# Mixer projections one weight tile at a time in one bank each, neighbourhood scores in the projections' banks, products of two heads side by side

## The chip, the cores and the metric

The kernel runs on one core of a Trainium2 chip. The metric is the device time of one execution in microseconds (us); the figure for a kernel is the median of several executions. One further execution is taken by the hardware profiler, and all views of the trace come from it.

## The reference: what is computed

Two layers of a macaron encoder over 512 tokens of width 1024, in float32: half a SwiGLU step, a mixer, half a SwiGLU step, and a last RMSNorm. Only the mixer is touched by the change. It projects the normalised input once, splits the result, and runs two groups of heads side by side: eight heads of neighbourhood attention (NA) on an 8 x 64 grid with a learned bias, and four heads of gated linear attention (GLA) in both directions.

```python
def hybrid_layer(x, ...):
    x = x + 0.5 * swiglu(rmsnorm(x, ffn1_norm), ffn1_wg, ffn1_wu, ffn1_wd)
    h = rmsnorm(x, mix_norm)
    proj = h @ w_in
    na_q, na_k, na_v, g_q, g_k, g_v, g_r, gf_code, gb_code = jnp.split(proj, offsets, axis=-1)
    na_o = neighbourhood_attention(split_heads(na_q, NA_HEADS), split_heads(na_k, NA_HEADS),
                                   split_heads(na_v, NA_HEADS), na_rpb)
    na_o = rmsnorm(merge_heads(na_o), na_gain)
    ...
    o_fwd = gla_chunked(qg, kg, vg, log_gf, True)
    o_bwd = flip(gla_chunked(flip(qg), flip(kg), flip(vg), flip(log_gb), False))
    gla_o = rmsnorm(o_fwd + o_bwd, gla_gain).astype(x.dtype)
    gla_o = merge_heads(gla_o) * jax.nn.silu(g_r)
    x = x + jnp.concatenate([na_o, gla_o], axis=-1) @ w_out
    x = x + 0.5 * swiglu(rmsnorm(x, ffn2_norm), ffn2_wg, ffn2_wu, ffn2_wd)
    return x
```

## The kernel before

A float32 product is made of three passes (`mm3`): weights and activations are split into a high and a low part, and high by high, high by low and low by high are added up in one PSUM bank. ACT rounds the high part of a weight tile (L149, the tile `wh`), DVE subtracts it to get the low part (L150, `wl`), and the matmuls stand on lines L169 to L171. Moving tiles are 512 tokens wide.

Each layer runs FFN 1, the mixer and FFN 2 one after the other. In the mixer, `mixer` builds four streams and hands them to `interleave`, which steps through generators: each step yields a price and a delay, or the name of a result that it waits for, and the stream that is due first is stepped next. This gives the instructions a priority; a list scheduler then puts every engine's instructions in their order when the program is built. The four streams are `gla_all(0)` and `gla_all(1)` (two GLA heads each), `na_all` (eight units of NA, two heads by half the queries each) and `fillers`: the projections of the remaining eleven pairs of 128-column weight tiles in the order of `PAIRS`, then the NA half of the output projection (`op_part`, eight chunks).

`fillers` are the large products, 128x128 weights by 512 columns, that keep TensorE busy while the other streams wait for ACT and DVE. A pair is made by `dmat_steps`: two weight tiles in two banks of the tag "mm", their k-steps alternating, or by `vmat_steps` for the NA values, whose rows are tokens. When the last k-step of both is issued, `posts[...]` evacuates both banks. The tag "mm" is a ring of four PSUM banks, used for projections, for the sum of `gla_out` and for the output projection; the tag "sc" is a ring of two banks, used for the scores of GLA and of NA.

The small products take part of the array. GLA scores are 16 products of 64x64 for two heads (L630, two passes each, so 32 matmul records), 8 of 64x128 at n=128 (L701) and two blocks of 4 at n=256 (L715). A unit of NA takes 4 products of 64x128 at n=256 for its scores (L853), bias, row maximum and sum on DVE, exponentials on ACT (L865), four transposes (L876), and 8 products of 128x64 with the values (L887, P·V below). The values are copied to `M_v` with a scale per token (L808) and shifted copies `M_vm` are made of them (L813, L814). `gla_out` sums a GLA head (L769 to L773), squares and copies the bank on ACT (L776, L777), sums the squares over partitions on TensorE (L236, L237), and multiplies by the root and by Silu of the gate `gr` (L744) on DVE. The last chunks of the output projection carry tile names with OP.

Of the kernel before, what the change touches and what calls it, by code (L numbers as in the profile page):

```python
# [13 lines left out]
ALU = mybir.AluOpType  # L14
# [49 lines left out]
def trunk_kernel(ctx, tc, xin, wgu, wdn, win, wcode, wgate, wout, vec, rpbt,  # L64
# [102 lines left out]

    def mm3(ps, wh, wl, rh, rl, first, last, more=False):
        PE.matmul(ps, wh, rh, start=first, stop=False, skip_group_check=more)  # L169
        PE.matmul(ps, wh, rl, start=False, stop=False, skip_group_check=more)  # L170
        PE.matmul(ps, wl, rh, start=False, stop=last, skip_group_check=more)  # L171

# [150 lines left out]
    def dload(src, eng):  # L323
        raw = wp.tile([P, 2048], F32, tag="wraw", name=nm("wraw"))
        for q in (1, 0, 2, 3):
            qs = slice(q * T, (q + 1) * T)
            eng.dma_start(raw[:, qs], src[:, qs])
# [205 lines left out]
    def mixer(l):  # L533
# [58 lines left out]
        def post_gqk(pr):  # L592
            def post(ok, oq, r):
                for key, o in (("gk", ok), ("gq", oq)):
                    t = got[key, pr] = sl(key)
                    V.tensor_tensor(seq_out(t), unit_in(o), unit_in(r), op=ALU.mult)
            return post

        def gla_levels(pr):
# [49 lines left out]
            for li, h in enumerate((1, 2, 4, 8, 16, 32, 64, 128)):  # L649
# [45 lines left out]
                elif h2 == 128:  # L695
                    pss = psum("sc"), psum("sc")
                    for s in range(4):
                        t = s ^ 1
                        kk, qq = (KF, QF) if s < t else (KB, QB)
                        for hh in range(2):  # L700
                            PE.matmul(pss[hh][:, s * P:(s + 1) * P], kk[rows[hh], s * P:(s + 1) * P],  # L701
                                      qq[rows[hh], t * P:(t + 1) * P], start=True, stop=True)
# [4 lines left out]
                else:  # L707
                    for half in range(2):
# [3 lines left out]
                        for j in range(2):  # L712
                            s = 2 * half + j
                            for hh in range(2):
                                PE.matmul(pss[hh][:, j * 256:(j + 1) * 256],  # L715
                                          kk[rows[hh], s * P:(s + 1) * P], qq[rows[hh], o:o + 256],
                                          start=True, stop=True)
# [5 lines left out]
        def post_gv(h0):  # L723
            def post(o1, o2, r):
                vts = sl("vt"), sl("vt")
                for vt, o in zip(vts, (o1, o2)):
                    V.tensor_tensor(seq_out(vt), unit_in(o), unit_in(r), op=ALU.mult)

                def turn():
                    for hd, vt in zip((h0, h0 + 1), vts):  # L730
                        pt = psum("tp")
                        for i in range(4):
                            PE.transpose(pt[:, i * P:(i + 1) * P], vt[:, i * P:(i + 1) * P], idn)
                        got["gv", hd] = sl("gv")
                        S.activation(got["gv", hd], pt, AF.Copy)
# [3 lines left out]
        def post_gr(h0):  # L739
            def post(o1, o2, r):  # L740
# [12 lines left out]
        def gla_out(hd, tag):  # L753
            g = gla[hd // 2]
            hh = hd % 2
            yield ("gr", hd)
# [31 lines left out]
        def vmat_steps(pss, src, tags):  # L788
# [3 lines left out]
            pss += [psum(tag) for tag in tags]  # L792
            for t in range(4):
                ps = pss[t // 2][:, (t % 2) * H2:(t % 2 + 1) * H2]
                ts = slice(t * P, (t + 1) * P)
# [355 lines left out]
```

## Time and profile before

| | |
|---|---|
| median of 3 executions | 1952.68 us (1950.92 to 1956.05) |
| the profiled execution | 1957.23 us, of which the span of instructions 1955.5 us |
| busy share of the span | TensorE 98%, its weight loads 86%, VectorE 72%, ScalarE 52%, GpSimd 1% |
| mixer of layer 0 | about 370 to 630 us |
| mixer of layer 1 | about 1337 to 1600 us |

TensorE's matmuls are pipelined, so the busy time of one is longer than the distance to the next one; the distance of two starts is what a matmul costs. The granted clock of TensorE is given as a share of its full rate. All rows are in the section below the change.

### The profile page before, as it was taken

What the parts mean: (1) busy time and instruction counts of PE and PEld (TensorE: products, weight loads), DVE (VectorE), ACT (ScalarE), POOL (GpSimd) and SP (SyncE); (2) the same over time, 40 slices, a digit from 0 to 9 for tenths busy, and PEclk for the clock granted to TensorE, in tenths of its full rate; (3) what the DMA queues carried; (4) which work ended last, traced back from release to release, by engine and by line L of the source; (5) the groups of instructions that cost most, each with busy time, mean ns of one, the idle gap of its engine ahead of it and who ended that gap; (6) DMA issues with size and microseconds to landing.
All of it is one profiled execution on the core that took longest, in us unless ns stands there. A gap on an engine that the chain in (4) does not pass through costs nothing.

```text
span 1955.5 us, 32220 instructions
## 1 busy us (share of the span) xinstructions
PE 1924.7 (98%) x12490; PEld 1687.4 (86%) x12490; DVE 1416.9 (72%) x2705; ACT 1020.1 (52%) x1959; POOL 17.4 (1%) x36
## 2 busy tenths in 40 slices
PE   8999999999998999999999999999999999999997
PEld 7889989888777898999889899988887778999896
DVE  6958768676558875967788596776764689679585
ACT  5535536465564553644555364455654655546364
POOL 0000000000000000000000000000000000000000
PEclk9999999999999999999999999999999899999999
DMA  4333223322202332332223333232221033233322
GB/s 154 112 108 108 89 106 124 110 67 98 66 31 85 102 108 89 106 108 103 83 98 106 108 109 107 88 119 96 96 86 55 21 120 107 89 107 109 108 76 76
DMA packets 58249, 187.78 MB, mean 96 GB/s; under 512 B 6640, under 2 KB 13296, under 8 KB 45808
## 3 DMA queue, kind: packets, MB, share of 16 engines
q1 hardware_dynamic: 29904, 132.07, 19.8%
q10 hardware_dynamic: 25632, 45.27, 7.0%
q0 software_dynamic: 2560, 8.39, 1.3%
q8 instruction: 98, 1.61, 0.3%
q14 instruction: 55, 0.45, 0.1%
HBM read 183.60 MB, written 2.10 MB: 95 GB/s over the span
## 4 chain that ended last, share of the span: by engine, by line
PE 97%; DVE 1%; DMA 1%; ACT 1%; issue 0%; DVEq 0%; ACTq 0%
PE F_mm L169 14%; PE F_mm L171 14%; PE F_mm L170 14%; PE F_sc L169 9%; PE F_sc L170 9%; PE F_sc L171 9%; PE M_mm L169 6%; PE M_mm L170 6%; PE M_mm L171 6%; PE M_o L887 1%; PE M_sc L630 1%; PE M_tp L876 1%; PE M_sc L853 1%; PE M_mm L773 1%; PE M_sc L715 1%; DMA wraw<-in_wgu 0%
## 5 line engine op out<-in xcount | busy, mean ns | idle before, releaser
L149 ACT ACTIVATE F_wh<-F_wraw 128x512 fp32r<-128x512 f32 (+1 forms) x472 | 289.5, 617 | 439.9 <-PE F_sc L170 238.8
L169 PE MATMUL F_mm<-F_xc,F_wh 128*128 128x256 f32 x1792 | 500.5, 282 | 1.3 <-ACT F_wh L149 1.3
L170 PE MATMUL F_mm<-F_xc,F_wh 128*128 128x256 f32 x1792 | 501.5, 282 | 0.0
L171 PE MATMUL F_mm<-F_xc,F_wl 128*128 128x256 f32 x1792 | 495.2, 282 | 0.0
L150 DVE TENSOR_TENSOR F_wl<-F_wraw,F_wh 128x512 fp32r<-128x512 f32 (+1 forms) x472 | 312.8, 668 | 151.9 <-ACT F_wh L149 143.4
L169 PEld LDWEIGHTS F_mm<-F_xc,F_wh 128*128 128x128 f32 x1792 | 339.3, 190 | 3.7 <-ACT F_wh L149 1.9
L170 PEld LDWEIGHTS F_mm<-F_xc,F_wh 128*128 128x128 f32 x1792 | 340.3, 190 | 1.9
L171 PEld LDWEIGHTS F_mm<-F_xc,F_wl 128*128 128x128 f32 x1792 | 335.8, 190 | 0.0
L169 PE MATMUL F_sc<-F_hid,F_wh 128*128 128x512 f32 (+1 forms) x716 | 275.6, 387 | 1.3 <-DVE xt L455 1.3
L170 PE MATMUL F_sc<-F_hid,F_wh 128*128 128x512 f32 (+1 forms) x716 | 276.6, 386 | 0.0
L171 PE MATMUL F_sc<-F_hid,F_wl 128*128 128x512 f32 (+1 forms) x716 | 276.4, 386 | 0.0
L149 ACT ACTIVATE F_wh<-F_ws 128x512 fp32r<-128x512 f32 x256 | 161.8, 632 | 170.0 <-PE F_mm L170 109.8
L150 DVE TENSOR_TENSOR F_wl<-F_ws,F_wh 128x512 fp32r<-128x512 f32 x256 | 174.8, 688 | 41.8 <-ACT F_wh L149 38.8
L169 PEld LDWEIGHTS F_sc<-F_hid,F_wh 128*128 128x128 f32 x716 | 134.6, 188 | 29.0 <-DVE xt L455 3.0
L171 PEld LDWEIGHTS F_sc<-F_hid,F_wl 128*128 128x128 f32 x716 | 134.5, 188 | 26.4
L170 PEld LDWEIGHTS F_sc<-F_hid,F_wh 128*128 128x128 f32 x716 | 134.6, 188 | 25.7
L455 DVE SCALAR_TENSOR_TENSOR xt<-F_sc,xt 128x512 f32<-128x512 f32 x94 | 65.0, 691 | 96.7 <-PE F_sc L171 96.1
L169 PE MATMUL M_mm<-F_xd,M_wh 128*128 128x512 f32 x304 | 122.1, 403 | 0.0
L171 PE MATMUL M_mm<-F_xd,M_wl 128*128 128x512 f32 x304 | 120.3, 397 | 0.0
L170 PE MATMUL M_mm<-F_xd,M_wh 128*128 128x512 f32 x304 | 119.9, 395 | 0.0
L150 DVE TENSOR_TENSOR M_wl<-M_wraw,M_wh 128x512 fp32r<-128x512 f32 (+1 forms) x112 | 73.4, 669 | 35.9 <-ACT M_wh L149 32.4
L149 ACT ACTIVATE M_wh<-M_wraw 128x512 fp32r<-128x512 f32 (+1 forms) x112 | 67.6, 614 | 46.8 <-PE M_mm L170 37.9
(325 smaller groups left out, 3153.0 us busy)
## 6 DMA issues: line engine op xcount, KB each, us to landing
F_wraw<-in_wgu SPq DMA_DIRECT2D x64, 1024.0 KB, 4.7
F_wraw<-in_wdn SPq DMA_DIRECT2D x32, 1024.0 KB, 4.9
M_wraw<-in_win ACTq DMA_DIRECT2D x88, 256.0 KB, 3.6
F_wraw<-in_wgu ACTq DMA_DIRECT2D x80, 256.0 KB, 3.8
F_wraw<-in_wdn SPq DMA_DIRECT2D x16, 768.0 KB, 4.3
M_pp<-in_rpbt POOLq DMA_DIRECT2D x32, 256.0 KB, 3.1
M_wraw<-in_wout SPq DMA_DIRECT2D x16, 256.0 KB, 2.7
xt<-in_xin SPq DMA_DIRECT2D x8, 256.0 KB, 5.2
```

What stands on the lines that cost most here:

```text
L149: S.activation(h, src, AF.Copy)
L150: V.tensor_tensor(l, src, h.bitcast(F32), op=ALU.subtract)
L169: PE.matmul(ps, wh, rh, start=first, stop=False, skip_group_check=more)
L170: PE.matmul(ps, wh, rl, start=False, stop=False, skip_group_check=more)
L171: PE.matmul(ps, wl, rh, start=False, stop=last, skip_group_check=more)
L455: V.scalar_tensor_tensor(xt[:, c, :], pss[j], 0.5, xt[:, c, :], ALU.mult, ALU.add)
L630: PE.matmul(pss[hh][o:o + 64, (i // 2) * 64:(i // 2 + 1) * 64], *op(hh, i), start=True, stop=True)
L715: PE.matmul(pss[hh][:, j * 256:(j + 1) * 256], kk[rows[hh], s * P:(s + 1) * P], qq[rows[hh], o:o + 256], start=True, stop=True)
L773: PE.matmul(dst, vs(2 * half + j), fa[:, o:o + P], start=False, stop=(j == 1))
L853: PE.matmul(sco[hh][:, jj * 256:(jj + 1) * 256], q[rows[hh], j * P:(j + 1) * P], krhs, start=True, stop=True)
L876: PE.transpose(pt[:, i * P:(i + 1) * P], pp[:, i * P:(i + 1) * P], idn)
L887: PE.matmul(po[rows[hh], j * P:(j + 1) * P], v[:, rows[hh]], pps[hh][:, (jj * 2 + c) * P:(jj * 2 + c + 1) * P], start=(c == 0), stop=(c == 1))
```

## The change

Five things change in the mixer.

- `paired` is new: it issues the products of two heads in turn, head 1 then head 0, and asks for program order for all but the first of a group. GLA scores, NA scores and P·V go through it, so in the new file their matmuls all stand on L171, and `mm3` on L176 to L178.
- The NA scores take two banks of the tag "mm" in place of "sc".
- Projections go by `tile_steps`: 24 matmuls of one weight tile in one bank, which is evacuated at once by `done`, then the other tile. The pieces of a weight tile are fetched in another order. `vmat_steps` also works bank by bank. The prices of a step are 1.36 and 1.5 in place of 1.28.
- The posts handle one tile each. Silu of both gates comes when the second is there, and `gla_out` waits for a new key "gs".
- The wait of NA for the values moves from the start of a unit to just before its P·V.

```diff
+    def paired(mms):
+        for i, (ps, lhs, rhs, kw) in enumerate(mms):
+            ins = PE.matmul(ps, lhs, rhs, **kw)
+            if i:
+                tc.keep_in_program_order(ins)
...
-    def dload(src, eng):
+    def dload(src, eng, order=(1, 0, 2, 3)):
...
             def blocks(pss, op):
-                for i in range(8):
-                    o = (i % 2) * 64
-                    for hh in range(2):
-                        PE.matmul(pss[hh][o:o + 64, (i // 2) * 64:(i // 2 + 1) * 64], *op(hh, i),
-                                  start=True, stop=True)
+                paired([(pss[hh][i % 2 * 64:i % 2 * 64 + 64, (i // 2) * 64:(i // 2 + 1) * 64], *op(hh, i), SS)
+                        for i in range(8) for hh in (1, 0)])
...
         def post_gr(h0):
-            def post(o1, o2, r):
-                for hd, o in ((h0, o1), (h0 + 1, o2)):
-                    g = got["gr", hd] = sl("gr")
-                    V.tensor_tensor(g, o, r, op=ALU.mult)
-                    S.activation(g, g, AF.Silu)
-                lnexp()
+            def post(i, o, r):
+                g = got["gr", h0 + i] = sl("gr")
+                V.tensor_tensor(g, o, r, op=ALU.mult)
+                if i == 1:
+                    for hd in (h0, h0 + 1):
+                        S.activation(got["gr", hd], got["gr", hd], AF.Silu)
+                    lnexp()
+                    got["gs", h0] = got["gs", h0 + 1] = True
...
-        def vmat_steps(pss, src, tags):
+        def vmat_steps(src, done):
...
+        def tile_steps(src, done):
+            raw = dload(src, nc.scalar, (1, 2, 0, 3))
+            for j, qs in enumerate(((1, 2), (0, 3))):
+                w = [wsplit(raw[:, q * T:(q + 1) * T]) for q in qs]
+                ps = psum("mm")
+                for c in range(KD):
+                    h, l_ = w[c % 2]
+                    cs = slice(c // 2 * P, (c // 2 + 1) * P)
+                    mm3(ps, h[:, cs], l_[:, cs], *XD[c], c == 0, c == KD - 1)
+                    if c == KD - 1:
+                        done(j, ps)
+                    if c % 2:
+                        yield 1.36, 0.0
...
         def na_unit(hp, jp, pps, ctxd):
-            sco = psum("sc"), psum("sc")
+            sco = psum("mm"), psum("mm")
...
+            paired([(sco[hh][:, jj * 256:(jj + 1) * 256],
+                     q[rows[hh], (2 * jp + jj) * P:(2 * jp + jj + 1) * P], keys(hh, 2 * jp + jj), SS)
+                    for jj in range(2) for hh in (1, 0)])
...
             if jp == 0:
+                yield ("v", hp)
                 ctxd["po"] = psum("o")
...
+            paired([(po[rows[hh], j * P:(j + 1) * P], got["v", hp][VSEL[j][c]][:, rows[hh]],
+                     pps[hh][:, (j % 2 * 2 + c) * P:(j % 2 * 2 + c + 1) * P], dict(start=c == 0, stop=c == 1))
+                    for j in (2 * jp, 2 * jp + 1) for c in range(2) for hh in (1, 0)])
...
                     yield ("qk", u // 2)
-                    yield ("v", u // 2)
...
-                steps = (vmat_steps if a in ("v0", "v2") else dmat_steps)(bk, win[l, i], ("mm", "mm"))
+                steps = vmat_steps if a in ("v0", "v2") else tile_steps
```

The orders below are those of the two built programs; a row is an instruction, `xN` counts repetitions.

TensorE before, where the projections of a layer end (tiles 5800 and 5801 are the last two, `F_xd` is the mixer's input, 5762 is the P·V sum of the last NA heads):

```order
L170 MATMUL M_mm_5801<-F_xd_3834,M_wh_5823 128x512
L171 MATMUL M_mm_5801<-F_xd_3834,M_wl_5824 128x512
L630 MATMUL M_sc_5700<-M_ga_4630 64x64 x8
L630 MATMUL M_sc_5701<-M_ga_4630 64x64 x8
L876 MATMUL M_tp_5734<-con,M_pp_5501 128x128 x4
L701 MATMUL M_sc_5865<-M_ga_4630 128x128 x4
L701 MATMUL M_sc_5866<-M_ga_4630 128x128 x4
L876 MATMUL M_tp_5750<-con,M_pp_5503 128x128 x4
L887 MATMUL M_o_5762<-M_pp_5501,M_vm_4993 64x128
L715 MATMUL M_sc_6005<-M_ga_4630 128x256 x2
```

TensorE after, at the end of the P·V of the last NA heads (5643 there):

```order
L171 MATMUL M_o_5643<-M_pp_5390,M_v_4992 64x128
L171 MATMUL M_o_5643<-M_pp_5388,M_v_4992 64x128
L176 MATMUL M_mm_5715<-F_xd_3605,M_wh_5707 128x512
L177 MATMUL M_mm_5715<-F_xd_3605,M_wh_5707 128x512
L178 MATMUL M_mm_5715<-F_xd_3605,M_wl_5708 128x512
L176 MATMUL M_mm_5715<-F_xd_3611,M_wh_5711 128x512
```

Before, the last NA unit, the last GLA scores and the sums of all four GLA heads stand behind the last projection; after, tile 5715 and three more tiles (5784, 5842 and 5995), 96 matmuls in all, stand behind the last P·V.

TensorE after, the first NA unit's P·V inside a group of GLA scores (4510 and 4509 are the score banks of two GLA heads, 4484 is the first P·V sum):

```order
L171 MATMUL M_sc_4510<-M_ga_4167,M_kt_4402 64x64
L171 MATMUL M_sc_4509<-M_ga_4167,M_kt_4402 64x64
L171 MATMUL M_o_4484<-M_pp_4090,M_vm_4452 64x128
L171 MATMUL M_o_4484<-M_pp_4088,M_vm_4452 64x128
L171 MATMUL M_o_4484<-M_pp_4090,M_vm_4452 64x128
L171 MATMUL M_o_4484<-M_pp_4088,M_vm_4452 64x128
L171 MATMUL M_sc_4510<-M_ga_4167,M_kt_4402 64x64
L171 MATMUL M_sc_4509<-M_ga_4167,M_kt_4402 64x64
```

ACT after, ahead of the shifted values 4452 that these P·V products read (4343 is the bank of the values):

```order
L907 ACTIVATE M_pp_4116<-M_tp_4430 128x512
L336 DMA M_wraw_4882<-in_win 128x512
L149 ACTIVATE M_wh_4698<-M_wraw_4693 128x512
L336 DMA M_wraw_4882<-in_win 128x512
L895 ACTIVATE M_pp_4309,M_sm_4412<-M_pp_4309,M_sm_4412 128x256 x2
L895 ACTIVATE M_pp_4311,M_sm_4418<-M_pp_4311,M_sm_4418 128x256 x2
L832 ACTIVATE M_v_4337<-M_mm_4343,rcol 128x128
L832 ACTIVATE M_v_4338<-M_mm_4343,rcol 128x128
L832 ACTIVATE M_v_4337<-M_mm_4343,rcol 128x128
L832 ACTIVATE M_v_4338<-M_mm_4343,rcol 128x128
L149 ACTIVATE M_wh_4702<-M_wraw_4693 128x512
L840 ACTIVATE M_vm_4452<-M_v_4337 64x384
```

A group of 16 is cut in two by P·V, four products of which read shifted values that ACT makes behind the exponentials of the next NA unit.

TensorE before, the end of the last `gla_out` (6133) and the output projection chunk behind it:

```order
L769 MATMUL M_mm_6133<-M_at_5723,M_gv_5686 128x128
L770 MATMUL M_mm_6133<-M_am_5877,M_gv_5686 128x128
L773 MATMUL M_mm_6133<-M_af_6013,M_gv_5686 128x128 x2
L236 MATMUL M_tp_6112<-M_sqh_6113,onr 128x512
L237 MATMUL M_tp_6112<-M_sql_6114,onr 128x512
L169 MATMUL M_mm_6154<-M_oh_5004,M_wh_6157 128x512
```

TensorE after, at the same place (6089 is the last GLA head there):

```order
L772 MATMUL M_mm_6089<-M_at_5683,M_gv_5744 128x128
L773 MATMUL M_mm_6089<-M_am_5815,M_gv_5744 128x128
L776 MATMUL M_mm_6089<-M_af_5898,M_gv_5744 128x128 x2
L176 MATMUL M_mm_6110<-M_oh_4684,M_wh_6113 128x512
L177 MATMUL M_mm_6110<-M_oh_4684,M_wh_6113 128x512
```

Before, three chunks of the NA half of the output projection (12 matmuls each) stand ahead of the last `gla_out` and five behind it; after, one stands ahead and seven behind.

The number of matmuls is the same. Counted per layer in the two orders, the runs of small products, unbroken by others, go from 39 to 45, and the stretches of one kind from 46 to 55: of the 16 groups of 64x64 products four are cut in two, of the blocks of 64x128 at n=256 four halves with one head alone become pairs and five other blocks are cut, the two blocks at n=128 are cut 1 to 7, and of the eight P·V six are cut in both programs. ACT's table loads go from 20 to 30 in the whole program, five more in each mixer.

## Rows read from the trace of the kernel before

**Rows 1.** The page: busy time of each engine, and the chain that ended last.

```profile
PE 1924.7 (98%) x12490; PEld 1687.4 (86%) x12490; DVE 1416.9 (72%) x2705; ACT 1020.1 (52%) x1959; POOL 17.4 (1%) x36
...
PE 97%; DVE 1%; DMA 1%; ACT 1%; issue 0%; DVEq 0%; ACTq 0%
```

**Rows 2.** Stretches: from:to, length, busy PE, PEld, DVE, ACT, POOL, clock, DMA, GB/s.

```profile
430.00:546.00 116.00, 116.00 (x1007) 90.28 (x1006) 73.39 (x223) 64.35 (x149) 5.35 (x10) 1.00 0.22 73
546.00:565.00 19.00, 16.94 (x129) 12.74 (x128) 8.69 (x18) 12.54 (x25) 0.00 (x0) 0.82 0.17 56
565.00:583.00 18.00, 18.00 (x121) 16.31 (x120) 8.39 (x14) 12.07 (x21) 0.00 (x0) 1.00 0.05 16
583.00:597.00 14.00, 10.98 (x58) 9.18 (x57) 14.00 (x25) 5.48 (x11) 0.00 (x0) 0.88 0.03 11
615.00:630.00 15.00, 12.49 (x47) 9.59 (x47) 13.57 (x23) 9.97 (x18) 0.00 (x0) 0.89 0.31 107
...
555.00:560.00 5.00, 5.00 (x27) 3.53 (x28) 0.98 (x3) 2.25 (x4) 0.00 (x0) 0.50 0.00 0
...
1513.00:1531.00 18.00, 16.58 (x130) 12.60 (x129) 8.12 (x17) 12.37 (x25) 0.00 (x0) 0.81 0.18 60
1549.00:1563.00 14.00, 10.98 (x57) 9.15 (x57) 14.00 (x26) 5.34 (x10) 0.00 (x0) 0.88 0.05 11
1582.00:1600.00 18.00, 16.90 (x74) 13.31 (x73) 17.80 (x29) 14.46 (x25) 0.00 (x0) 1.00 0.43 139
```

**Rows 3.** TensorE's waits, 370 to 645 us: total, times, longest.

```profile
PE M_mm L169 <- ACT M_on L777: 3.0, 1, 3.0
PE OP_mm L171 <- DVE OP_wl L150: 2.3, 1, 2.3
PE M_sc L701 <- ACT M_at L693: 2.1, 2, 1.6
```

**Rows 4.** Timeline of TensorE: start, us, line, tile, records; first P·V, last projection.

```profile
445.65 0.66 PE L887 MATMUL M_o<-M_pp,M_v 128*64 128x128 f32 x8
...
548.37 0.39 PE L171 MATMUL M_mm<-F_xd,M_wl 128*128 128x512 f32 x1
```

**Rows 5.** Timeline of TensorE: small products between large ones.

```profile
419.62 0.39 PE L171 MATMUL M_mm<-F_xd,M_wl 128*128 128x512 f32 x1
419.94 0.72 PE L630 MATMUL M_sc<-M_ga,M_kt 64*64 64x64 f32 x32
420.59 0.50 PE L169 MATMUL M_mm<-F_xd,M_wh 128*128 128x512 f32 x1
420.93 0.39 PE L170 MATMUL M_mm<-F_xd,M_wh 128*128 128x512 f32 x1
...
425.26 0.39 PE L171 MATMUL M_mm<-F_xd,M_wl 128*128 128x512 f32 x1
...
499.51 0.43 PE L887 MATMUL M_o<-M_pp,M_v 128*64 128x128 f32 x2
499.87 0.50 PE L171 MATMUL M_mm<-F_xd,M_wl 128*128 128x512 f32 x1
...
526.94 1.13 PE L715 MATMUL M_sc<-M_ga 64*128 64x256 f32 x4
528.00 0.50 PE L171 MATMUL M_mm<-F_xd,M_wl 128*128 128x512 f32 x1
...
561.27 1.14 PE L715 MATMUL M_sc<-M_ga 64*128 64x256 f32 x8
562.35 0.66 PE L733 MATMUL M_tp<-con,M_vt 128*128 128x128 f32 x4
```

**Rows 6.** Timeline of ACT: values copied and shifted, then four exponentials.

```profile
413.96 0.37 ACT L808 ACTIVATE M_v<-M_mm,rcol 128x128 f32<-128x128 f32 x1
...
414.97 0.65 ACT L149 ACTIVATE M_wh<-M_wraw 128x512 fp32r<-128x512 f32 x1
...
415.64 0.52 ACT L814 ACTIVATE M_vm<-M_v 64x384 f32<-64x384 f32 x1
...
417.66 0.51 ACT L865 ACTIVATE M_pp<-M_pp,M_sm 128x256 f32<-128x256 f32 x1
...
419.56 0.19 ACT L865 ACTIVATION_READ_ACCUMULATOR M_pp<-M_pp,M_sm 128x1 f32 x1
```

**Rows 7.** One tile, M_sc: DVE's pass over NA scores, ns min/median/max.

```profile
L860 DVE CUSTOM_DVE_ANT_0 M_pp<-M_sc,M_pp x64: 415/420/425, 415.0 to 1508.6; 128x256 f32<-128x256 f32 x64
```

**Rows 8.** Timeline of ACT: a table load between two activations.

```profile
564.65 1.28 ACT L744 ACT_TABLE_LOAD   x1
565.94 1.15 ACT L744 ACTIVATE M_gr<-M_gr 128x512 f32<-128x512 f32 x2
```

More of the change, by code (lines that the diff above doesn't have):

```diff
@@ L321, in run @@
             pass
-    def dload(src, eng):
+    def dload(src, eng, order=(1, 0, 2, 3)):
         raw = wp.tile([P, 2048], F32, tag="wraw", name=nm("wraw"))
-        for q in (1, 0, 2, 3):
+        for q in order:
             qs = slice(q * T, (q + 1) * T)
@@ L711, in gla_levels @@
                         o = 256 * (1 - half)
[L712 to L717, printed above, removed]
+                        paired([(pss[hh][:, j * 256:(j + 1) * 256],
+                                 kk[rows[hh], (2 * half + j) * P:(2 * half + j + 1) * P], qq[rows[hh], o:o + 256], SS)
+                                for j in range(2) for hh in (1, 0)])
                         for hh in range(2):
@@ L723, in post_gv, with post @@
         def post_gv(h0):
-            def post(o1, o2, r):
-                vts = sl("vt"), sl("vt")
-                for vt, o in zip(vts, (o1, o2)):
-                    V.tensor_tensor(seq_out(vt), unit_in(o), unit_in(r), op=ALU.mult)
+            def post(i, o, r):
+                vt = sl("vt")
+                V.tensor_tensor(seq_out(vt), unit_in(o), unit_in(r), op=ALU.mult)
                 def turn():
[L730 to L735, printed above, removed]
+                    pt = psum("tp")
+                    for b in range(4):
+                        PE.transpose(pt[:, b * P:(b + 1) * P], vt[:, b * P:(b + 1) * P], idn)
+                    got["gv", h0 + i] = sl("gv")
+                    S.activation(got["gv", h0 + i], pt, AF.Copy)
                 return turn
@@ L802, in post_v @@
-        def post_v(t0):
-            def post(b0, b1, r):
-                vas = sl("v"), sl("v")
-                for t in range(4):
-                    src = (b0, b1)[t // 2][:, (t % 2) * H2:(t % 2 + 1) * H2]
+            for b in range(2):
+                ps = psum("mm")
+                for t in (2 * b, 2 * b + 1):
+                    po = ps[:, (t % 2) * H2:(t % 2 + 1) * H2]
+                    ts = slice(t * P, (t + 1) * P)
+                    for c in range(KD):
+                        cs = slice((c % 2) * H2, (c % 2 + 1) * H2)
+                        mm3(po, *(a[:, ts] for a in XD[c]), *(a[:, cs] for a in w[c // 2]), c == 0, c == KD - 1)
+                        if c % 4 == 3:
+                            if t % 2 and c == KD - 1:
+                                done(b, ps)
+                            yield 1.5, 0.0
@@ L807, in post @@
+        def post_v(t0):
+            vas = []
+            def post(b, o, r):
+                if b == 0:
+                    vas.extend((sl("v"), sl("v")))
+                for t in (2 * b, 2 * b + 1):
+                    src = o[:, (t % 2) * H2:(t % 2 + 1) * H2]
                     for i, va in enumerate(vas):
```

81 lines of the change are left out of this document (35 added, 46 removed).

## The prediction, made before the changed kernel ran

> **What bounds the kernel now.** The page comes first: TensorE is busy for 98% of the span and carries 97% of the chain that ended last [rows 1]. So the time is TensorE's work plus the few places where it stands still or runs slowly. I then cut the two mixers into stretches and looked in each for idle time and for a clock below 1.00 [rows 2]. From 430 to 546 us TensorE is busy for 116.00 of 116.00 us at clock 1.00: in the long middle, where large projections lie between all small work, nothing can be won but work itself. Three places in a mixer lose time. I price each as the idle time plus the length times the missing share of the clock.
>
> A, 546 to 565 us: idle 19.00 - 16.94 = 2.06, clock 0.82, so 0.18 x 19 = 3.42; together 5.5 us. Layer 1, 1513 to 1531 us: 1.42 + 0.19 x 18 = 4.8 us. Both: 10.3 us. The matmuls of L701 wait for ACT's score copies, 2.1 us in two waits [rows 3], and then the clock falls to 0.50 for five us although TensorE is never idle in them [rows 2]; a 2.4 GHz engine runs at 1.2 there. The last projection starts at 548.37 us [rows 4]: from there only small products and transposes are left, each waiting for the other engines.
>
> B, 583 to 597 us and 1549 to 1563 us: 3.02 + 0.12 x 14 = 4.7 us in each layer, 9.4 us in all. A chunk of the output projection waits 3.0 us for a bank that ACT has still to copy out behind the last `gla_out` [rows 3], and VectorE is busy for 14.00 of 14.00 us there [rows 2]: ACT stands behind VectorE's chain of gains and roots.
>
> C, the end of the output projection: 615 to 630 us loses 2.51 + 0.11 x 15 = 4.2 us, 1582 to 1600 us 1.1 us; 5.3 us in all. The longest wait is for the low part of a weight tile, made by VectorE [rows 3], which is busy for 13.57 of 15 and 17.80 of 18 us [rows 2].
>
> Together 25.0 us, 1.3% of the run, is what better cover in the mixers can give at most.
>
> **The change part by part.** *Cover moved to the end.* NA no longer waits for the values before a unit starts, and a weight tile is evacuated alone, so the order after starts NA earlier and has four projection tiles, 96 matmuls, left behind the last P·V, where before there were none. Large matmuls follow each other at (425.26 - 420.93) / 19 = 0.228 us [rows 5], so that is 21.9 us of work that waits for nothing late, spread through stretch A, 19 us long. A's two waits were for ACT, 12.54 us busy in 19.00 [rows 2]; with 21.9 us laid in, ACT is ahead. I take the whole of A: -10.3 us (bounds 0 and -10.3).
>
> Of the output projection's NA half seven chunks of 12 matmuls follow the last `gla_out` instead of five, 84 x 0.228 = 19.2 us against 13.7, and another chunk lies between the last two heads, so that the ring's next bank is asked for later. The wait of 3.0 us in B has 5.5 us more cover behind the head, and the two heads are separated by 12 x 0.228 = 2.7 us. I take the whole of B: -9.4 us (bounds 0 and -9.4). C has the same VectorE work under more matmuls, but its last chunks depend on the last head as before; I take half: -2.7 us (bounds 0 and -5.3).
>
> *Pairs.* Does program order of the two heads save anything by itself? Four products of one head take 528.00 - 526.94 = 1.06 us, eight of both heads 562.35 - 561.27 = 1.08 us [rows 5], and in that block the heads came as head, head, other, other. So two heads run side by side whenever both stand in one block; alternation adds nothing, and only the four halves of L715 that stood alone gain: four halves become two blocks, 2 x 1.06 = 2.1 us per layer. Against it stand the cuts. Entering a run of small products costs (419.94 - 419.62) - 0.228 = 0.09 us, leaving it (420.93 - 420.59) - 0.228 = 0.11 us [rows 5], 0.20 in all. Six more runs: 1.2 us. The block prices summed over the pieces of both orders (a whole group of 16 is 0.65 us by rows 5; one product of P·V alone costs 499.87 - 499.51 = 0.36, and little goes off the rest) give 38.1 us before and 39.0 after, the 2.1 us already in it, so +0.9. Together +2.2 per layer, +4.5 us in both (bounds 0, if the cuts cost no more than the halves gave, and 9, twice that).
>
> *A new wait: the first P·V.* Before, 32 us lay between the first copy of a value, at 413.96 us, and its first use, at 445.65 [rows 4, 6]. After, TensorE comes to P·V with shifted values 30 large matmuls (6.8 us), two sets of four transposes, four other P·V products and twelve GLA products after the NA scores whose exponentials are queued on ACT ahead of the values: some 9.2 us. In that time VectorE needs some 2.4 us for bias and row maxima (four passes of 0.42 us [rows 7] and their small steps), ACT 419.75 - 417.66 = 2.1 us for four exponentials, 415.64 - 413.96 = 1.7 us for four copies and a rounding, 2 x 0.52 = 1.0 us for two shifts [rows 6]: 7.2 us. With an empty VectorE there is no wait; with up to 5 us queued on it (two low parts and six to eight updates of GLA factors stand ahead in its order) the wait is 7.2 + 5 - 9.2 = 3.0 us. VectorE is 63% busy in the middle stretch (73.39 of 116 [rows 2]), so I take 2 us per layer, 4 us in all; bounds 0 and 2 x (3.0 + 3.4), 3.4 being what the clock cost in A. Behind the waiting P·V stand four pinned GLA scores and then six matmuls of a projection.
>
> *ACT's tables.* Ten more table loads. One starts at 564.65 us and the activation behind it at 565.94 [rows 8]: 1.29 us, 6.4 us per mixer. Between the last P·V and the GLA half of the output projection ACT would have some 35 us of work by the durations of the trace, these loads among it, in 50 us of TensorE work, so they cost nothing while that cover lasts; if it is gone, they come straight onto B. The Trainium skill, ScalarE: Activation LUTs, What ACT_TABLE_LOAD costs, gives 2.66 us for a switch of tables, since a drain of 1.38 us comes on top of the load. By it five loads would take 13.3 us per mixer, and ACT 42 of 50 us. The trace disagrees: the activation starts 0.01 us after the load has ended.
>
> *Rest.* The NA scores in "mm" take two of four banks for about as long as VectorE's passes; the projection then has two banks and uses one at a time. The order of the four pieces of a weight tile changes nothing in what is moved, and TensorE never waits for such a transfer [rows 3]. Both are taken at nothing; a projection that did wait would show as idle time with clock loss, the price of the slow rival below. The feed-forward parts are untouched.
>
> **The sum.** -10.3 - 9.4 - 2.7 + 4.5 + 4 = -13.9 us. The profiled execution took 1957.23 us (span 1955.5, 1.73 outside), which gives 1943.3. It lies 4.55 us above the median of the three executions, 1952.68 us; since the losses are of the same places in any execution, I take the difference from the median: 1938.8, rounded 1939.
>
> **The rivals.** *More comes back:* A, B and C vanish and the cuts are paid by the pairs: -25.0, some 1928. For it: static work in the middle shows no loss now. Against: six more runs and VectorE's load in C.
>
> *B and C stay:* -10.3 + 4.5 + 4 = -1.8, about 1951. VectorE is full in both places now [rows 2], the same VectorE work follows the last head, and five table loads lengthen ACT's chain. Against it: seven chunks of cover where five were short by 3 us.
>
> *The pinned groups stall (slower):* eight score groups per layer have their first product alone, then large matmuls or transposes, then the rest, which cannot be overtaken. The second head's bank may come free later than the first's, and TensorE waits with everything queued behind. A's two waits cost 5.5 us with the clock, 2.75 each. 13.9 / 2.75 = 5 such waits in the run eat the gain; from 8 on the kernel is slower. With five in each layer: -13.9 + 10 x 2.75 = +13.6, 1966. Against it: none of the stretches between 430 and 546 us shows such a wait now, though the ring of two banks was shared by more work then.
>
> **How the numbers follow.** About 0.3%, 5.9 us, is what can be told from no change. The forecast has 0.55, its own range 1933 to 1945; more comes back 0.17; B and C stay 0.15; the pinned groups stall 0.13. So faster 0.72, same 0.15, slower 0.13. The range reaches from 1927, the full gain, to 1957, beyond the third case and into the smallest losses, and leaves out most of the slow rival and little below.
>
> **What will show it.** Right: in stretch A of the new trace, matmuls of projections between the last scores, TensorE without idle time and at clock 1.00; the wait for L777's successor gone; two waits of 1 to 3 us at the first P·V. Pairs: blocks of both heads still at 1.06 us, no group shorter than before. Wrong: idle time of TensorE in the middle stretch behind a first product on L171, a clock of 0.50 there, or the 3 us wait at the last head still present; also if the median moves while these places don't.

## The result and the profile after

The changed kernel takes 1934.2 us (median of four executions, 1933.62 to 1934.72), the kernel before 1953.7 us beside it (1950.92 to 1956.05). The ratio is 0.9897, 95% interval 0.9885 to 0.9909: 1.0% faster, 19.5 us by the medians. The prediction was 1939 us with a range of 1927 to 1957. The profiled execution takes 1934.52 us, its span is 1932.7 us, 22.8 us less than the span before; the profiled execution before lay above its median, which is why the spans differ by more than the medians.

The page of the kernel after, busy time by engine and the chain that ended last (against [rows 1]):

```profile
PE 1913.4 (99%) x12490; PEld 1676.8 (87%) x12490; DVE 1412.2 (73%) x2705; ACT 1031.3 (53%) x1969; POOL 17.4 (1%) x36
...
PE 98%; DVE 1%; DMA 1%; ACT 0%; issue 0%; DVEq 0%; ACTq 0%
```

Stretches of the kernel after (from:to, length, busy PE, PEld, DVE, ACT, POOL, clock, DMA, GB/s). The end of a mixer has moved up by 13.4 us in layer 0 and by 23.0 us in layer 1 (its last matmul starts at 620.75 and 1574.22 us, before at 634.18 and 1597.19), so a stretch at the end must move along to hold the same work: 606 to 621 and 1559 to 1577 us are the ends of the two output projections, 347 to 621 and 1301 to 1574.5 the two mixers whole.

```profile
430.00:546.00 116.00, 116.00 (x1013) 89.66 (x1012) 74.72 (x213) 69.25 (x150) 4.31 (x8) 1.00 0.22 72
546.00:565.00 19.00, 19.00 (x121) 15.53 (x120) 3.80 (x7) 12.09 (x18) 0.00 (x0) 1.00 0.14 41
583.00:597.00 14.00, 14.00 (x63) 11.60 (x62) 14.00 (x26) 3.91 (x8) 0.00 (x0) 1.00 0.15 47
606.00:621.00 15.00, 14.32 (x63) 11.21 (x62) 14.77 (x25) 13.18 (x22) 0.00 (x0) 1.00 0.40 134
347.00:621.00 274.00, 273.32 (x1953) 218.90 (x1952) 185.64 (x448) 162.61 (x326) 5.37 (x10) 1.00 0.23 76
1500.00:1520.00 20.00, 20.00 (x131) 16.79 (x132) 4.97 (x8) 13.51 (x21) 0.00 (x0) 1.00 0.11 36
1535.00:1549.00 14.00, 14.00 (x63) 11.60 (x62) 14.00 (x26) 4.80 (x11) 0.00 (x0) 1.00 0.15 45
1559.00:1577.00 18.00, 17.43 (x76) 13.79 (x75) 17.83 (x30) 15.08 (x25) 0.00 (x0) 1.00 0.50 165
1301.00:1574.50 273.50, 272.93 (x1951) 218.56 (x1950) 185.49 (x447) 162.56 (x326) 5.36 (x10) 1.00 0.23 76
```

Where [rows 2] had a clock of 0.82, 0.88 and 0.89 and idle time of two to three microseconds, TensorE now runs at clock 1.00 from one end of a mixer to the other, and all its idle time, 0.7 and 0.6 us, lies at the end of the output projection. VectorE is still busy for 14.00 of 14.00 us from 583 to 597 us, and TensorE does not wait there. The table of TensorE's waits from 370 to 645 us has one row in place of those of [rows 3]:

```profile
PE OP_mm L176 <- ACT OP_wh L149: 0.6, 1, 0.6
```

**A sum that closes.** For every kernel below two numbers were worked out. *Work* is TensorE's order in one mixer, up to the end of the output projection, priced block by block: 0.2268 us for a 512-wide product, 0.12 for a 256-wide one, 0.109 for a transpose, the prices of small blocks as in the prediction, 0.20 for entering and leaving a run of them. It needs only the order and the prices of the trace before. *Lost* is what the starts of the matmuls in the kernel's own trace take beyond these prices in both mixers: waits, low clock, and wherever a price was wrong.

| kernel | work per mixer | lost, both | span | median |
|---|---|---|---|---|
| before | 231.5 | 35.7 | 1955.5 | 1953.7 to 1955.8 |
| after | 233.8 | 7.4 | 1932.7 | 1934.2 |
| e1_v_wait | 235.8 | 12.5 | 1940.9 | 1943.1 |
| e2_prices | 232.1 | 18.4 | 1939.6 | 1941.4 |
| e3_cover_only | 232.1 | 15.2 | 1936.5 | 1936.6 |
| e4_old_prices | 232.0 | 7.3 | 1928.4 | 1930.2 |
| e5_not_pinned | 230.6 | 7.4 | 1923.9 | 1927.2 |
| e6_head_by_head | 231.8 | 23.9 | 1944.3 | 1946.4 |
| e7_two_banks | 232.7 | 14.0 | 1933.8 | 1935.8 |
| e8_one_bank_alone | 225.0 | 35.3 | 1940.9 | 1943.7 |
| e9_heads_off_ring | 231.5 | 26.0 | 1946.9 | 1948.4 |
| e10_scores_in_sc | 235.5 | 24.5 | 1951.5 | 1952.9 |
| e11_values_early | 231.0 | 16.8 | 1935.5 | 1937.8 |
| e12_not_pinned_1_42 | 228.4 | 10.5 | 1923.7 | 1923.9 |

Span less twice the work less what is lost is 1454.4 to 1457.9 us in all fourteen. That it closes is in part so by construction, because what is lost is read from the starts of the same trace: the rest is the time outside the mixers, and the table shows that this rest does not change. So the change is told by two numbers: it adds 2 x 2.3 = 4.6 us of work and takes away 28.3 us of lost time. Their difference is 23.7 us, the spans differ by 22.8, so they hold to about a microsecond. No kernel here loses less than 7.3 us; of the 7.4 us of the changed kernel 1.25 us are idle time (the two rows above), and the rest was not taken apart.

### The profile page after: what moved, and what is told of

Same layout as the page of the kernel before. It is cut to its first block, busy times and chain, and to the rows that moved or that the text cites. A ratio compares the mean times of both kernels' runs of the same rounds, so it can differ in the third digit from the quotient of the medians.

```text
span 1932.7 us, 32200 instructions
## 1 busy us (share of the span) xinstructions
PE 1913.4 (99%) x12490; PEld 1676.8 (87%) x12490; DVE 1412.2 (73%) x2705; ACT 1031.3 (53%) x1969; POOL 17.4 (1%) x36
## 4 chain that ended last, share of the span: by engine, by line
PE 98%; DVE 1%; DMA 1%; ACT 0%; issue 0%; DVEq 0%; ACTq 0%
PE F_mm L176 14%; PE F_mm L178 14%; PE F_mm L177 14%; PE F_sc L176 9%; PE F_sc L178 9%; PE F_sc L177 9%; PE M_mm L176 6%; PE M_mm L178 6%; PE M_mm L177 6%; PE M_sc L171 2%; PE M_o L171 1%; PE M_mm L171 1%; PE M_tp L906 1%; PE M_mm L776 1%; DMA wraw<-in_wgu 0%; PE F_tp L176 0%
## 5 line engine op out<-in xcount | busy, mean ns | idle before, releaser
L176 PE MATMUL F_mm<-F_xc,F_wh 128*128 128x256 f32 x1792 | 500.7, 282 | 1.7 <-ACT F_wh L149 1.7
L178 PE MATMUL F_mm<-F_xc,F_wl 128*128 128x256 f32 x1792 | 494.9, 282 | 0.0
L176 PEld LDWEIGHTS F_mm<-F_xc,F_wh 128*128 128x128 f32 x1792 | 339.3, 190 | 4.3 <-ACT F_wh L149 2.5
L178 PEld LDWEIGHTS F_mm<-F_xc,F_wl 128*128 128x128 f32 x1792 | 335.6, 190 | 0.0
L176 PE MATMUL F_sc<-F_hid,F_wh 128*128 128x512 f32 (+1 forms) x716 | 275.6, 387 | 1.3 <-DVE xt L464 1.3
L178 PE MATMUL F_sc<-F_hid,F_wl 128*128 128x512 f32 (+1 forms) x716 | 276.4, 386 | 0.0
L176 PEld LDWEIGHTS F_sc<-F_hid,F_wh 128*128 128x128 f32 x716 | 134.5, 188 | 28.9 <-DVE xt L464 3.0
L178 PEld LDWEIGHTS F_sc<-F_hid,F_wl 128*128 128x128 f32 x716 | 134.5, 188 | 26.6
L176 PE MATMUL M_mm<-F_xd,M_wh 128*128 128x512 f32 x304 | 124.4, 409 | 0.0
L178 PE MATMUL M_mm<-F_xd,M_wl 128*128 128x512 f32 x304 | 119.6, 393 | 0.0
```

## The experiments

Medians are of four executions or more each; where two variants are compared, the ranges of their executions do not overlap unless it is said. The split posts, the key "gs" and the order in which the pieces of a weight tile are fetched were not tried alone; e3 has none of them.

### One part of the change alone

**The wait for the values** (e1), in the kernel before:

```diff
                     yield ("qk", u // 2)
-                    yield ("v", u // 2)
...
             if jp == 0:
+                yield ("v", hp)
                 ctxd["po"] = psum("o")
...
```

> The kernel before with one part of the change: NA waits for the values just before P.V, not at the start of a unit. In its order some 82 projection matmuls (before none) stand behind the last P.V, but four chunks of the output projection, not three, stand ahead of the last gla_out. Theory 1 (the gain is cover in stretches A and B, nothing else): stretch A is cured, B stays or grows; -10 to -12 us against before, some 1942 us, TensorE at clock 1.00 from 540 to 565 us, and a wait of 3 us or more for ACT's copy of the bank behind the last gla_out. Rival (banks freed one at a time and paired heads carry the gain): no more than -3 us, 1951.

Measured: 1943.14 us, ratio 0.9938 (0.9921 to 0.9954). The number was met and the reason only half: A is gone, but so is B, and the order has 4.3 us more work per mixer, 46 runs of small products against 39. Its only wait in layer 0 is new, at the first chunk that needs a GLA head's result:

```profile
PE M_mm L169 <- ACT M_oh L152: 1.7, 1, 1.7
```

**The prices** (e2), in the kernel before:

```diff
-                    yield 1.28, 0.0
+                    yield (1.5 if a in ("v0", "v2") else 1.36), 0.0
```

> The kernel before with one part of the change: the prices of a projection's step, 1.36 and 1.5 in place of 1.28, nothing else. In its order one chunk of the output projection instead of three stands ahead of the last gla_out, so seven follow it; the last NA unit's P.V still stands behind the last projection. Theory 1: B is cured, A stays for the most part: -9 to -11 us, some 1944 us; no wait for L777. Rival (banks and pairs): no change, 1953.

Measured: 1941.41 us, ratio 0.9929 (0.9914 to 0.9944). Again a number close to the one expected, with the places changed over: A is cured and B is not. The stretches of A and B in e2, the matmul that waits in B, and ACT's queue in front of the copy that it waits for:

```profile
546.00:565.00 19.00, 19.00 (x150) 15.96 (x149) 8.11 (x14) 14.36 (x24) 0.00 (x0) 1.00 0.16 56
582.00:600.00 18.00, 16.02 (x70) 13.25 (x71) 18.00 (x33) 6.34 (x13) 0.00 (x0) 1.00 0.09 30
```

```profile
583.99 0.50 PE L169 MATMUL M_mm<-M_oh,M_wh 128*128 128x512 f32 x1 [2.41 <-ACT M_on L777]
```

```profile
579.38 0.69 ACT L242 ACTIVATE M_r<-M_tp,vecs 128x512 f32<-128x512 f32 x1 [0.65 <-PE M_tp L237]
...
581.61 0.69 ACT L242 ACTIVATE M_r<-M_tp,vecs 128x512 f32<-128x512 f32 x1 [0.57 <-PE M_tp L237]
...
582.86 0.58 ACT L776 ACTIVATE M_sq<-M_mm 128x512 f32<-128x512 f32 x1
583.34 0.59 ACT L777 ACTIVATE M_on<-M_mm 128x512 f32<-128x512 f32 x1
```

The last head's sum was complete at about 574.5 us, and seven chunks of output projection follow it. ACT comes to its bank 8.4 us later (L776, then the copy L777), because two roots that wait for TensorE's own column sums (L237) stand ahead of it in ACT's order. One of the next chunks takes the head's bank, however many chunks there are: in the built order the third one here, behind 24 matmuls or 5.4 us of work, and in the kernel before the very next one (tile 6154 lies in the bank of 6133). So the number of chunks behind the last head, on which the prediction had based B, is not what hides this copy, but the number that lie ahead of the one that takes its bank.

**Cover without pairs and without single banks** (e3): e1 and e2 together, and the NA scores in "mm", in the kernel before:

```diff
-            sco = psum("sc"), psum("sc")
+            sco = psum("mm"), psum("mm")
```

> The kernel before with three parts of the change, none of which is a pair of heads or a projection in one bank: the wait for the values just before P.V, the NA scores in the ring of four banks, and the prices 1.36 and 1.5. In its order 96 projection matmuls stand behind the last P.V and one chunk ahead of the last gla_out, as in the changed kernel. Theory 1: the whole gain, -18 to -22 us, 1932 to 1936 us. Rival: at most half, 1944 or more.

Measured: 1936.64 us (1936.21 to 1938.30), ratio 0.9906 (0.9891 to 0.9921). Up to the first matmul of the last four chunks the mixers are a microsecond shorter than those of the changed kernel (258.1 against 259.1 us from the first matmul of the projections); what is missing to it is lost at the end of the output projection, 4.1 and 3.5 us, where it waits for the parts of weight tiles. Neither pairing nor single banks are needed for nearly all of the gain.

**Projections in one bank alone** (e8): the changed kernel without program order, NA scores in "sc", the values' wait at the start.

> Of the change only the projections in one bank each with their prices and posts: no program order for pairs, NA scores in the ring of two banks, the wait for the values at the start of a unit. In its order 24 projection matmuls stand behind the last P.V and one chunk of the output projection ahead of the last gla_out; only 31 runs of small products per layer, 225.0 us of work. Theory 2: if no wait comes back, 8.8 us less work per layer than the changed kernel, some 1917 us; with the wait for L777 back in each layer (4.7 us each) 1926. Rival (the gain is the NA scores in the ring of four and the values' wait): 1945 or more.

Measured: 1943.69 us, ratio 0.9941 (0.9927 to 0.9956): 18 to 27 us slower than expected. The order has the least work of all, since small products are gathered in 31 runs, and it loses 35.3 us. Stretch A is back: between 531 and 559 us TensorE has nothing but small products, transposes and the GLA sums, and by the price of idle time plus missing clock it loses 28.00 - 23.34 + 0.12 x 28 = 8.0 us there. That 24 projection matmuls stand behind all of them helps nothing. The stretch, and the longest of TensorE's waits in it:

```profile
531.00:559.00 28.00, 23.34 (x236) 19.01 (x233) 12.84 (x37) 19.95 (x41) 0.00 (x0) 0.88 0.06 20
```

```profile
PE M_sc L171 <- ACT M_at L696: 2.1, 1, 2.1
```

### One part of the change taken back

**The old prices** (e4), 1.28 in place of 1.36 and 1.5 in the changed kernel.

> The changed kernel with the old prices of a projection's step, 1.28 for all. In its order the cover behind the last P.V is kept (102 matmuls), but four chunks of the output projection stand ahead of the last gla_out instead of one. Theory 1: A stays cured, B is back with its 4.7 us per layer or a little more: +9 to +11 us against the changed kernel, some 1944 us, and a wait for the bank behind the last gla_out in the trace. Rival: as the changed kernel, 1934.

Measured: 1930.22 us (1929.35 to 1932.09), ratio 0.9873 (0.9858 to 0.9888): not 10 us slower than the changed kernel but 4 us faster. There are four chunks ahead of the last head and no wait for the copy of its bank (L777 before, L780 here) at all; the four that follow do run short, by 0.7 us, at the first use of a head's result:

```profile
PE M_mm L176 <- ACT M_oh L152: 0.7, 1, 0.7
```

With e2 this turns the prediction's reading of B round: few chunks behind the last head give a wait for `M_oh`, which has to come through VectorE's chain (0.7 us with 48 matmuls ahead of the head here, 1.7 in e1 with 48, 2.7 in e7 with 57); the wait for the bank is another matter. The 1.8 us less work per mixer account for nearly all of the 4 us.

**NA scores back in "sc"** (e10), one line of the changed kernel.

> The changed kernel with the NA scores back in the ring of two banks, shared with GLA. In its order nine groups of small products and transposes follow each other without a large matmul between them, from the last but one NA scores to the GLA sums, and the last tile of the projections stands behind them; 235.5 us of work per layer against 233.8. Theory 2 (A is lost where no large matmul lies BETWEEN the dependent small steps, wherever the last projection stands): A is back with some 9 us per layer as in the kernel with one-bank projections alone, and 1.7 us of work: +21 us, some 1955 us. Rival (24 matmuls behind the last P.V are cover enough): +3 us, 1938.

Measured: 1952.88 us, ratio 0.9984 (0.9974 to 0.9993). Nearly the whole gain is gone, as expected: 2.9 us are left against the kernel before beside it (1955.78 us, 1953.55 to 1958.18), and the ranges of the two touch. Two of its stretches, and the timeline of TensorE in them:

```profile
551.00:556.00 5.00, 2.91 (x19) 1.83 (x18) 4.01 (x10) 4.62 (x11) 0.00 (x0) 0.88 0.00 0
556.00:561.00 5.00, 5.00 (x20) 3.53 (x20) 4.17 (x8) 2.96 (x5) 0.00 (x0) 0.50 0.00 0
```

```profile
552.02 0.48 PE L171 MATMUL M_sc<-M_ga 64*128 64x128 f32 x2 [0.92 <-DVE M_ga L677]
553.11 1.16 PE L171 MATMUL M_sc<-M_ga 64*128 64x128 f32 x14 [0.61 <-ACT M_at L698]
...
556.31 2.08 PE L171 MATMUL M_sc<-M_ga 64*128 64x256 f32 x8
558.32 1.11 PE L734 MATMUL M_tp<-con,M_vt 128*128 128x128 f32 x4
```

Several waits of under a microsecond, and then a group of four products for two heads at n=256 that takes 558.32 - 556.31 = 2.01 us instead of 1.08, at clock 0.50: stretch A again. With two banks for all scores the last P·V ends at 549 us, 21 us later than in the changed kernel, and of the projections only one tile is left by then, which stands behind the first GLA sums.

**The values' wait back at the start** (e11), one line of the changed kernel.

> The changed kernel with the wait for the values back at the start of an NA unit. In its order only 25 projection matmuls stand behind the last P.V, but large matmuls lie between all the last groups of small products; 231.0 us of work per layer against 233.8. Theory 2: no wait in the stretch before the GLA sums, -5 to -6 us, some 1929 us. Rival (the values' wait is what made the gain, as in the kernel with that part alone): A is back, 1945 or more.

Measured: 1937.80 us (1936.03 to 1939.17), ratio 0.9909 (0.9892 to 0.9925). No wait before the GLA sums, so the values' wait isn't needed once the scores have four banks; up to the last four chunks of the output projection the mixer is 1.3 us shorter than in the changed kernel. But 3.7 us per layer are lost at the end of the output projection, which no theory had foreseen:

```profile
PE OP_mm L178 <- DVE OP_wl L150: 1.7, 1, 1.7
PE OP_mm L176 <- ACT OP_wh L149: 1.2, 2, 0.7
```

**Projections in two banks again** (e7):

```diff
-                steps = vmat_steps if a in ("v0", "v2") else tile_steps
+                steps = vmat_steps if a in ("v0", "v2") else two
```

where `two` runs `dmat_steps` in two banks, at the old price of 1.28, and calls `done` for both at the last step.

> The changed kernel with the projections of queries, keys, GLA and gates again in two banks at a time, both evacuated at the end, at the old price of a step (the values still bank by bank). Cover behind the last P.V 102 matmuls, 57 matmuls of the output projection ahead of the last gla_out. Theory 2: work 232.7 us per layer against 233.8, so -2 us, 1932, with waits of under 1 us. Rival (freeing one bank at a time is what keeps the ring open for the NA scores): waits for banks in the middle of the mixer, 1940 or more.

Measured: 1935.80 us (1935.52 to 1938.23), ratio 0.9905 (0.9888 to 0.9921). No wait for a bank in the middle: single banks are not what keeps the ring open. The 2 us of work saved and more are lost again in the wait for `M_oh`, 2.7 us in each layer.

### Pairs

**Not held in program order** (e5), products still written head 1, head 0 in turn:

```diff
             ins = PE.matmul(ps, lhs, rhs, **kw)
-            if i:
-                tc.keep_in_program_order(ins)
```

> The changed kernel, products of two heads still written in turn, but no longer held in program order. In its order there are 39 runs of small products per layer, not 45, and the cover behind the last P.V and the last gla_out is the same. Theory 2 (with no idle time left, the time goes by TensorE's own work in the order, block by block): 230.6 us of work per layer in the stretch where the changed kernel has 233.8, so -6 us, some 1928 us. Rival (pinned pairs make the heads run side by side): slower than the changed kernel by 3 us or more, 1937.

Measured: 1927.23 us (1925.70 to 1928.97), ratio 0.9857 (0.9842 to 0.9872), 7 us below the changed kernel. The scheduler keeps the written turn by itself and cuts fewer groups. Holding the order costs what the sum of work said, 3.2 us per mixer.

**Head by head** (e6):

```diff
-        for i, (ps, lhs, rhs, kw) in enumerate(mms):
+        for i, (ps, lhs, rhs, kw) in enumerate(mms[::2] + mms[1::2]):
```

> The changed kernel with each pinned group written head by head: all products of head 1, then all of head 0, in program order. 39 runs of small products per layer. Theory 2: a whole group costs what it costs in alternation (8 records of L853's kind 1.06 us), the work is 231.8 us per layer, so -4 us, some 1930 us. Rival (alternation is what lets two heads overlap): every group takes up to twice its time, some 40 groups of 0.6 to 1.1 us per layer, +30 us a layer at most, at least +10 in all.

Measured: 1946.42 us (1945.46 to 1947.02), ratio 0.9954 (0.9940 to 0.9969): 12 us slower than the changed kernel, where 4 us faster was expected, and 19 us slower than e5, which has as many runs of small products. There is no new wait; the groups themselves are longer. A group of 16 products of 64x64 between two large ones, in e6 and then in e5:

```profile
399.12 0.97 PE L171 MATMUL M_sc<-M_gkq,M_gkq 64*64 64x64 f32 x32
400.03 0.50 PE L176 MATMUL M_mm<-F_xd,M_wh 128*128 128x512 f32 x1
```

```profile
397.68 0.69 PE L171 MATMUL M_sc<-M_gkq,M_gkq 64*64 64x64 f32 x32
398.30 0.50 PE L174 MATMUL M_mm<-F_xd,M_wh 128*128 128x512 f32 x1
```

0.91 us head by head, 0.62 in alternation. Groups of L701's kind take 1.64 against 1.10 us, P·V in runs of 12 to 16 records 0.2 to 0.5 us more. Only the groups at n=256 take 1.07 in either order, and it was from one of these, [rows 5], that the prediction had concluded.

### The ring, and a version that beats both

**The last two heads off the ring** (e9), one line of the kernel before:

```diff
-GOT = ('mm', 'mm')
+GOT = ('mm', 'o')
```

> The kernel before with one edit that isn't in the change: the sums of the last two GLA heads are put in the bank of P.V, which is free by then, not in the ring of four. TensorE's order is the same up to the third GLA head; no chunk of the output projection then needs a bank that ACT has still to copy. Theory 2 (B is the ring: after four banks a chunk meets the last but one head's bank, whose copy stands behind roots on ACT): the wait of 3.0 us for L777 and its clock loss go in both layers, -9 us, some 1945 us, if no later wait takes over; A stays with M_sc waiting for L693. Rival (VectorE, full there, is the bound, so the wait moves): at most -3 us, with a wait for M_oh or for a low part OP_wl of about the same length instead.

Measured: 1948.43 us (1947.66 to 1950.82), ratio 0.9964 (0.9951 to 0.9977): between the two. TensorE's waits from 540 to 640 us, and the stretch of B:

```profile
PE M_sc L701 <- ACT M_at L693: 2.6, 2, 2.1
PE M_mm L169 <- ACT M_oh L152: 1.9, 1, 1.9
PE M_mm L169 <- DVE M_on L950: 0.9, 1, 0.9
```

```profile
583.00:597.00 14.00, 13.12 (x74) 11.07 (x74) 13.90 (x25) 6.32 (x13) 0.00 (x0) 1.00 0.06 20
```

The wait for L777 is gone, with TensorE's order unchanged up to the third head: the stretch of B loses 0.9 us at clock 1.00, where it lost 4.7. So B was the ring. A is as before. Part of it comes back as a wait for the heads' results, probably because the chunks behind now start early and none is left later; that wasn't tried.

**Not held in order, with a price of 1.42** (e12): e5, and in `tile_steps`

```diff
-                        yield 1.36, 0.0
+                        yield 1.42, 0.0
```

> The changed kernel, not held in program order, and with 1.42 in place of 1.36 as the price of a projection's step: a version meant to beat both. 39 runs of small products and 44 stretches, 228.4 us of work per layer against 230.6 with the old price; large matmuls between all late groups; one chunk of the output projection ahead of the last head. Theory 2: -4 us against the unpinned kernel (1927), some 1923 us. Rival (what is saved in work comes back as waits): 1927 or more.

Measured: 1923.85 us (1921.94 to 1925.52), ratio 0.9837 (0.9822 to 0.9852): 10 us below the changed kernel. Against e5 the median is 3.4 us lower, but the spans are 1923.7 and 1923.9 us. By the table its mixers are 1.3 us shorter, 2.2 us less work in each and 3.1 us more lost in both; in the profiled execution that is evened out ahead of them, where its first projection starts at 348.44 us against 345.32 in e5, before anything that the edit touches. So e12 is ahead, by one to three microseconds.

## Why the prediction was right or wrong

**The direction, A and the clock: right.** A was predicted at -10.3 us and is gone in both layers at clock 1.00. What the row before had shown, that TensorE runs at half rate for some microseconds after short waits, is where much of the gain comes from: waits of 1.6 and 0.5 us were followed by five at clock 0.50, and of the 25.0 us priced from [rows 2] 11.9 are missing clock. The measure used for the cover was too coarse. Counting the projection matmuls behind the last P·V gave 96 against none, but e2 cures A with none and e8 has A with 24: what counts is whether large matmuls lie between the dependent small steps. Of the parts of the change it is the NA scores in the ring of four that do this in the changed kernel (e10 brings A back), while the values' wait or the prices alone do it in the kernel before (e1, e2). Each moves the order; none is necessary.

**B: the right size by a wrong step.** -9.4 us was predicted, and B is gone. The step "seven chunks of 12 matmuls follow the last `gla_out` instead of five" failed: e2 has seven and waits 2.4 us per layer, e4 has four and doesn't wait for this copy. Nor is a chunk between the last two heads new: one lies there in both orders. e9 shows the cause: a chunk takes the bank of a GLA head, and ACT copies that bank only behind roots that wait for TensorE. The last head's sum and the copy that is waited for, before:

```profile
586.31 0.61 PE L773 MATMUL M_mm<-M_af,M_gv 128*128 128x128 f32 x4
```

```profile
589.77 0.58 ACT L777 ACTIVATE M_on<-M_mm 128x512 f32<-128x512 f32 x1
```

That copy ends 3.4 us after the sum. In the changed kernel it is no quicker; it ends at 581.5 us, 5.4 us after the last head, while TensorE is busy with other chunks:

```profile
575.81 0.28 PE L776 MATMUL M_mm<-M_af,M_gv 128*128 128x128 f32 x1
575.84 0.47 PE L176 MATMUL M_mm<-M_oh,M_wh 128*128 128x512 f32 x1
```

```profile
580.91 0.59 ACT L780 ACTIVATE M_on<-M_mm 128x512 f32<-128x512 f32 x1
```

In its built order the fifth chunk behind the last head takes that bank, 48 matmuls or 10.9 us later, in both layers, where before it was the next one. That the change as a whole put the bank so far back was luck, as far as the prediction goes; which part of it did so was not taken apart (e2 moves the bank to the third chunk, e3 to the sixth).

**C: too small.** -2.7 us was predicted for both layers; by the same price it went from 5.3 to 0.68 + 0.57 = 1.25 us (606 to 621 and 1559 to 1577 us above), -4.0. Half had been taken for want of a reason. The variants don't give one either: with the same chunks and the same VectorE work, the end of the output projection loses between 0.9 us (e5) and 4.1 us (e3) per layer. What sets it stays open.

**The size of what is lost: the mis-sized term.** Idle time plus missing clock gave 25.0 us for A, B and C, of which 1.25 is left, so 23.75 have gone. Matmul by matmul the two mixers before lost 35.7 us, 28.3 more than after. The price by windows was too low by some 4 us; where in the windows they lie was not taken apart. This, the next term and C, 4.5, 4 and 1.3 us, are why the time came out below the forecast.

**The first P·V: no wait.** +4 us was predicted. ACT has the shifted values at 423.79 + 0.53 = 424.32 us, and TensorE comes for them 0.84 us later, behind the twelve GLA products, in the timelines of ACT and TensorE after:

```profile
423.24 0.52 ACT L840 ACTIVATE M_vm<-M_v 64x384 f32<-64x384 f32 x1
423.79 0.53 ACT L839 ACTIVATE M_vm<-M_v 64x384 f32<-64x384 f32 x1
```

```profile
424.65 0.58 PE L171 MATMUL M_sc<-M_ga,M_kt 64*64 64x64 f32 x24
425.16 0.66 PE L171 MATMUL M_o<-M_pp,M_vm 128*64 128x128 f32 x8
425.75 0.34 PE L171 MATMUL M_sc<-M_ga,M_kt 64*64 64x64 f32 x8
```

The lower bound of the term was the right end: VectorE, for which five microseconds of queue had been allowed, takes up the NA scores 0.3 us after their last product (TensorE's next instruction starts at 417.25 us):

```profile
417.56 0.42 DVE L890 CUSTOM_DVE_ANT_0 M_pp<-M_mm,M_pp 128x256 f32<-128x256 f32 x1
```

**Pairs: right in sum, wrong in reason.** +4.5 us was predicted for the cuts, the sum of work says +4.6, and e5 gets 7 us back by leaving the order free. "Alternation adds nothing" is refuted by e6 for all kinds but one. The kernel before had most groups in alternation without being held to it, so the error cost nothing in this sum; that too is luck.

**ACT's tables: right.** No wait of TensorE stands behind one of the ten loads; in the busiest place after, from the last two heads on, a load is again followed at once by its activation, 1.29 us from start to start:

```profile
562.70 1.28 ACT L252 ACT_TABLE_LOAD   x1
563.99 0.63 ACT L252 ACTIVATE M_r<-M_r 128x512 f32<-128x512 f32 x1
```

**The rivals.** "More comes back" (1928) was nearer in its mechanism than in its time: nearly all of A, B and C came back, but the cuts were not paid by the pairs. "B and C stay" didn't happen: both are down to the 1.25 us at the end. "The pinned groups stall" didn't happen: no first product on L171 waits in the middle, and holding the order costs work, not waits.

## What to carry to other kernels

Where one engine is busy for 98% of the time, add up its own work in the built order, block by block, and compare with the trace: over fourteen kernels the time outside the mixers stays within 3.5 us, and a variant's time follows from its order once its waits are known and its blocks are priced in the order in which they are issued (the same block prices were 16 us short for e6). Small dependent steps need long independent work between them, not behind them; look at what stands between, and take it for granted that a reordering for one reason will move the place of the last wait. Before holding instructions in an order, look whether the scheduler keeps it anyway: writing the heads in turn was worth having, holding the turn cost 7 us.

## What the runs showed that was not expected

Alternating the two heads is worth 0.29 us in a group of sixteen 64x64 products (0.91 against 0.62 us) and 0.54 us in eight of 64x128 at n=128 (1.64 against 1.10), and nothing at n=256 (1.07 against 1.06). In e10 the stretch at clock 0.50 follows five microseconds with 2.09 us of idle time, of which no single wait is longer than 0.92 us; before, the longest in A was 1.56 us. In e2 one wait of 2.41 us, with large matmuls on both sides, is followed by clock 1.00 (582 to 600 us). So the length of a single wait doesn't tell what the clock does after it.
